# A streaming encoder layer in exact float32 parts: weight parts kept in DRAM, and branch B's v normalised by two passes of the vector engine

## The chip, the core and the metric

The kernel runs on one core of one Trainium2 chip. The metric is the device time of one execution in microseconds (us), as the median of several runs. Five engines share the work of a core: PE multiplies matrices (its weight loads are listed apart, as PEld), DVE is the vector engine, ACT the scalar engine, POOL the GpSimd engine, and SP here only issues DMAs. Each runs its own list of instructions in the order in which the program gives them.

## The reference

One layer of an encoder runs over a new stream of 2048 frames and over eight running streams of 16 frames each, all of width 1024, in float32. What is computed, cut to what matters here:

```python
h = einsum('btd,de->bte', x, w_in)                     # 1024 -> 2816 columns
a, g_a, u, v, g_b, c1, c2, g_c = split(h)              # 256 256 384 384 384 384 384 384
y_a = pool_mixer(a)                                    # trailing means, 4 windows, 64 x 64 products
v_n = layer_norm(v, gmlp_ln_g, gmlp_ln_b)
y_b = u * spatial_mix(v_n, gmlp_w, gmlp_b)             # 4 heads, 128 x 128, lower triangle
c   = c1 * sigmoid(c2)
y_c = silu(layer_norm(conv31(c))) @ conv_pw_w + conv_pw_b    # causal, one filter a channel
mixed = concat(silu(g_a) * y_a, silu(g_b) * y_b, silu(g_c) * y_c)
x_new = layer_norm(2 ** 0.25 * x + mixed @ w_out + b_out)

def layer_norm(x, g, b):
    return (x - mean) * rsqrt(var + 1e-5) * g + b
```

The normalised rows of v of the running streams, and the last rows of a and c, are outputs too.

## The kernel before, in words

**Products in two parts.** PE's one-pass type holds fewer bits than float32. Each operand is therefore split into a high part, which is the cast, and a low part, which is what is left: `split` (L150) has ACT cast (L152), and DVE subtract 1.0 us later by the planner's time. A product is three matmuls (`mm3`, L183): high by high (L189), high by low and low by high (L190, L191).

**Tokens and groups.** The 2048 frames are 16 token tiles of 128; a 17th holds the eight running streams. Three blocks take 6, 6 and 5 of them. The split tokens of a block stay in SBUF (`xhi`, `xlo`; `XRow`, L212, loads and splits one k-tile of 128 rows). The 2816 columns of w_in are done in eight groups, in this order: two of c1 and c2, two of ga and a, then v, gb, u, gc. A group has three column tiles of 128 (those of ga and a two). So the weights of all eight groups are needed again in each block.

**Weights.** A group's weights come in four pieces of two k-tiles each (`Piece`, L166): a load from DRAM into one of four slots of the stage (L171), on SP's DMA queue, and then a split into one of six slots of the weight ring (`whi`, `wlo`). A `Loader` (L799) starts the loads of the next group while the present one runs. It splits the first pieces after 6 and 9 us of planned PE time and two more during the group's last product; each split frees a slot of the stage for the next load. This is done anew in every block. At the end of a block the tokens of the next one come through the same stage.

**Branch B.** For each token tile `b_v` (L627) makes v in PSUM, and `stats` (L363) takes mean and variance on DVE (`vst`, `vmv`). After 1.0 us POOL makes 1/sigma and -mean/sigma out of them (`rstd`, L376: `vrs` in L378 and L379, `vnm` in L381). After another 1.2 us ACT normalises from PSUM into `vn` (L385), and after 0.8 us more POOL multiplies by `vg` (L649) and adds `vb` (L650). Of three tiles together each of the four heads is split (`vhi` on ACT, `vlo` on DVE) and multiplied by the spatial weights (`ps_z`, L672). POOL later multiplies the results `zb` by the gate (L689), and `b_u` (L692) by u, with a transposition (`tp_b`, L706).

**Branch C.** The convolution is 31 taps for each channel tile on DVE, one instruction a tap (`acc`, 128 x 768). Its taps are filler: `run_fill` (L100) puts one into DVE's list wherever the planner's clock of DVE has fallen behind its clock of PE. A block's tail (mean, variance, pointwise product; L496) runs during the next block, and that of the last one during the output stage.

**Branch A** makes its differences on DVE and its 64 x 64 products with split weights (`poolwhi`, `poolwlo`), which are loaded once (L315).

**What sets the order.** Nothing is reordered: each engine runs its instructions as the program gives them (L87 to L131). `after(us, ...)` puts a step into the lists when the planner's clock of PE has come that far. All DVE work but a few steps at the start goes through one wrapper and carries the line L131; it is told apart by its tiles. SP's DMAs start in order too.

**Output stage.** The branches of a token tile are stored to DRAM (`mix`), loaded again and split (`Mixed`, L878), and multiplied by w_out (`WPart`, L898), which takes the place of the tokens. The first two token tiles go together, k by k (`ps_o`). POOL scales b_out (L926) and adds it to the residual rows `xr` (L947); DVE then adds `ps_o` to `xr`.

Of the kernel before, what the change touches and what calls it, by code (L numbers as in the profile page):

```python
# [9 lines left out]
F32 = mybir.dt.float32  # L10
# [15 lines left out]
# Column tiles of 128 of the input projection.  # L26
# [23 lines left out]

# Columns of the packed per-partition constants.
# [22 lines left out]
def encoder_kernel(ctx: ExitStack, tc: tile.TileContext, a):  # L74
# [29 lines left out]
    def drain(tag=None):  # L104
        """What is left of the convolution that `tag` names, or all of it."""
# [13 lines left out]
    class Vector:  # L119
        """The vector engine, with its time counted."""  # L120
# [27 lines left out]
    ring = {}  # L148

    def split(hi, lo, src, then=None):  # L150
        """src (float32) = hi + lo exactly, both in the tensor engine's one-pass type."""
# [14 lines left out]
    class Piece:  # L166
        """A load into the stage, and later its split into a piece of the weight ring."""
        def __init__(self, key, src, cols):
            self.key, self.n, self.cols = key, src.shape[1], cols
# [3 lines left out]
        def split(self, then=None):  # L173
# [3 lines left out]
            ring.setdefault(self.key, []).append((hi, lo))  # L177

# [4 lines left out]
    def mm3(outs, kdim=KT, hook=None):  # L183
        """outs: (ps, lhs, rhs); the products of both parts but for lo x lo, below float32's last bit."""
# [18 lines left out]
    def w_in(key, g):  # L203
        """The loads of a group's weights, to be made one by one."""
# [889 lines left out]
```

## Time and profile before

| | |
|---|---|
| median of 3 runs | 805.1 us (805.04 to 805.83) |
| span of the profiled execution | 802.9 us |
| the three runs' median less this span | 2.2 us |
| PE busy | 778.2 us, 97% |
| DVE busy | 659.0 us, 82% |
| ACT busy | 255.0 us, 32% |
| POOL busy | 216.7 us, 27% |
| DMA | 88.34 MB, 110 GB/s on average |

The profile is one execution, and its times count from the start of the span. A row for a single instruction gives its start, its length, the engine, the line, the operation with output and inputs, and in square brackets the idle time before it and the work that ended this idle time. A row with a count (x4) holds several alike that follow each other, with their busy time together. A row of a group gives count, busy time, mean length in ns and the idle time before its members. In a list of waits the engine that waited stands ahead of the arrow, and the one it waited for behind it. A busy share near 100% says that an engine is hardly ever without work; it does not say what its short pauses wait for.

### The profile page before, as it was taken

How to read it: one execution, taken by the hardware profiler on the slowest of the kernel's cores; microseconds unless marked ns; L12 is line 12 of the kernel's file. 1: busy time of each engine (PE TensorE's matmuls, PEld its weight loads, DVE VectorE, ACT ScalarE, POOL GpSimd, SP SyncE). 2: the span in 40 equal slices, each digit the busy share in tenths (PEclk: the TensorE clock that was granted, in tenths of full speed). 3: DMA queues.
4: the chain of work that ended last, by engine and by line, in shares of the span. 5: the costliest groups of instructions: out<-in, count | busy, mean ns of one | idle time of the engine just before them, and what ended most of it. 6: DMA issues, size and time to landing. Idle time of an engine off the chain costs nothing.

```text
span 802.9 us, 11388 instructions
## 1 busy us (share of the span) xinstructions
PE 778.2 (97%) x4340; PEld 734.9 (92%) x4340; DVE 659.0 (82%) x930; ACT 255.0 (32%) x457; POOL 216.7 (27%) x226
## 2 busy tenths in 40 slices
PE   8999998999999999989999999999999899999995
PEld 6999997999999999989999999999988678888885
DVE  5998989995588999999667888999777897676665
ACT  5313224314432241431354243442351233231210
POOL 1010077300002005731000201742009344232332
PEclk9999999999999999999999999999999999999998
DMA  7513311225501253111461134222575344425321
GB/s 244 162 53 109 100 60 57 64 66 170 165 28 53 73 133 97 60 40 59 136 199 47 54 83 129 83 69 86 159 236 203 124 138 158 158 108 177 121 79 64
DMA packets 50918, 88.34 MB, mean 110 GB/s; under 512 B 13616, under 2 KB 27440, under 8 KB 50864
## 3 DMA queue, kind: packets, MB, share of 16 engines
q1 hardware_dynamic: 50864, 87.62, 33.9%
q8 instruction: 34, 0.56, 0.3%
q14 instruction: 20, 0.16, 0.1%
HBM read 69.02 MB, written 18.58 MB: 109 GB/s over the span
## 4 chain that ended last, share of the span: by engine, by line
PE 70%; DVE 13%; POOL 6%; issue 4%; DMA 4%; ACT 2%; SPq 0%; POOLq 0%; DVEq 0%; ACTq 0%
PE ps_c L189 6%; PE ps_o L189 5%; PE ps_o L191 5%; PE ps_c L190 5%; PE ps_o L190 5%; PE ps_c L191 5%; DVE acc L131 4%; PE ps_u L191 3%; PE ps_u L189 3%; PE ps_u L190 3%; PE ps_gc L191 2%; PE ps_gc L189 2%; PE ps_gc L190 2%; PE ps_ga L190 2%; PE ps_ga L189 2%
## 5 line engine op out<-in xcount | busy, mean ns | idle before, releaser
L131 DVE SCALAR_TENSOR_TENSOR acc<-cext,cw,acc 128x768 f32<-128x768 f32 (+1 forms) x270 | 265.8, 984 | 4.0
L131 DVE TENSOR_TENSOR wlo<-stage,whi 128x768 fp32r<-128x768 f32 (+1 forms) x99 | 90.0, 919 | 15.8 <-ACT whi L152 15.4
L189 PE MATMUL ps_c<-xhi,whi 128*128 128x384 f32 (+1 forms) x288 | 96.1, 334 | 0.6 <-ACT xhi L152 0.6
L190 PE MATMUL ps_c<-xlo,whi 128*128 128x384 f32 (+1 forms) x288 | 94.7, 329 | 0.9 <-DVE xlo L131 0.9
L191 PE MATMUL ps_c<-xhi,wlo 128*128 128x384 f32 (+1 forms) x288 | 94.1, 327 | 0.0
L152 ACT CAST whi<-stage 128x768 fp32r<-128x768 f32 (+1 forms) x99 | 75.4, 773 | 25.3 <-PE ps_c L190 11.8
L191 PE MATMUL ps_o<-woxhi,mlo 128*128 128x512 f32 (+1 forms) x208 | 81.5, 392 | 1.8 <-DVE mlo L131 1.8
L189 PE MATMUL ps_o<-woxhi,mhi 128*128 128x512 f32 (+1 forms) x208 | 81.9, 394 | 0.0
L190 PE MATMUL ps_o<-woxlo,mhi 128*128 128x512 f32 (+1 forms) x208 | 80.7, 388 | 0.0
L440 POOL COPY halo_c<-cext 128x30 f32<-128x30 f32 x9 | 5.1, 567 | 213.4 <-DVE cext L131 213.4
L190 PEld LDWEIGHTS ps_c<-xlo,whi 128*128 128x128 f32 x288 | 54.4, 189 | 2.4 <-DVE xlo L131 2.4
L189 PEld LDWEIGHTS ps_c<-xhi,whi 128*128 128x128 f32 x288 | 54.5, 189 | 1.4 <-ACT xhi L152 1.2
L191 PEld LDWEIGHTS ps_c<-xhi,wlo 128*128 128x128 f32 x288 | 54.3, 189 | 0.0
L385 ACT ACTIVATE xr<-xr,onm,ors 128x1024 f32<-128x1024 f32 x16 | 19.9, 1244 | 106.3 <-POOL onm L381 106.3
L191 PEld LDWEIGHTS ps_o<-woxhi,mlo 128*128 128x128 f32 x208 | 39.4, 189 | 11.0 <-DVE mlo L131 2.2
L189 PE MATMUL ps_gc<-xhi,whi 128*128 128x384 f32 (+1 forms) x144 | 47.3, 328 | 0.0
L191 PE MATMUL ps_gc<-xhi,wlo 128*128 128x384 f32 (+1 forms) x144 | 47.0, 326 | 0.0
L190 PE MATMUL ps_gc<-xlo,whi 128*128 128x384 f32 (+1 forms) x144 | 46.9, 326 | 0.0
L190 PEld LDWEIGHTS ps_o<-woxlo,mhi 128*128 128x128 f32 x208 | 39.4, 190 | 8.1
L189 PE MATMUL ps_gb<-whi,xhi 128*128 128x384 f32 x136 | 46.8, 344 | 0.0
L189 PE MATMUL ps_u<-whi,xhi 128*128 128x384 f32 x136 | 46.6, 343 | 0.0
L189 PEld LDWEIGHTS ps_o<-woxhi,mhi 128*128 128x128 f32 x208 | 39.6, 190 | 7.5
(188 smaller groups left out, 1967.1 us busy)
## 6 DMA issues: line engine op xcount, KB each, us to landing
stage<-in_w_in SPq DMA_DIRECT2D x71, 384.0 KB, 3.6
xr<-in_x_prompt SPq DMA_DIRECT2D x16, 512.0 KB, 4.9
o_y<-xr SPq DMA_DIRECT2D x16, 512.0 KB, 2.9
stage<-mix SPq DMA_DIRECT2D x17, 384.0 KB, 4.0
stage<-in_w_in SPq DMA_DIRECT2D x24, 256.0 KB, 2.7
stage<-in_xT SPq DMA_DIRECT2D x14, 384.0 KB, 3.8
mix<-yt SPq DMA_DIRECT2D x17, 192.0 KB, 1.9
mix<-mixs SPq DMA_DIRECT2D x17, 192.0 KB, 2.1
```

Of the source, the lines that this page charges most:

```text
L131: return fn(*args, **kw)
L152: nc.scalar.copy(hi, src)
L189: nc.tensor.matmul(ps, lh, rh, start=(k == 0), stop=False)
L190: nc.tensor.matmul(ps, lh, rl, start=False, stop=False)
L191: nc.tensor.matmul(ps, ll, rh, start=False, stop=(k == kdim - 1))
L385: nc.scalar.activation(out=out, in_=src, func=AF.Identity, scale=rs, bias=nm_)
L440: nc.gpsimd.tensor_copy(halo_c[:, j, :], ext[:, Tp:Tp + CONVC])
```

## The change

**Weights.** In block 0 everything is loaded and split as before, but 3 us (planned) after each split the two parts of the piece are also written to DRAM, into tiles named `keep` (`put`: two DMAs on SP, 64 in all). In blocks 1 and 2 a new class `Kept` loads the two parts from there, straight into the weight ring, or, for the first two pieces of every second group, into the stage, two slots a piece, from which PE then reads. Nothing is split there: 44 pieces of 768 columns and 16 of 512 go from ACT (cast) and DVE (subtraction). The loads are issued 5 to 8 us after the start of the group before, those that go into the stage after 10 and 11. Only the last group of the last block is still loaded from w_in and split.

**Tokens.** From block 0 to 1 the token rows still come through a `Loader`; from block 1 to 2 they are loaded during the last products of the block and split partly after its last group.

**v.** On DVE, right behind the statistics, a first pass takes (v - mean) times `vg` from PSUM into `vn`. POOL makes only 1/sigma (`inverse`). After 2.4 us a second pass, on DVE, multiplies by 1/sigma and adds `vb`. ACT's normalisation (17 instructions), POOL's -mean/sigma (17) and POOL's two passes (34) go; DVE has 34 more instructions of 128 x 384.

Since the planner counts DVE's work, taps move into the room that the subtractions leave.

```diff
     class Piece:
-        def __init__(self, key, src, cols):
-            self.key, self.n, self.cols = key, src.shape[1], cols
+        def __init__(self, key, src, cols, keep=None):
+            self.key, self.n, self.cols, self.keep = key, src.shape[1], cols, keep
...
             ring.setdefault(self.key, []).append((hi, lo))
+            if self.keep is not None:
+                after(3, lambda: put(self.keep, hi, lo, self.cols))
+
+    def put(keep, hi, lo, cols):
+        for x, part in enumerate((hi, lo)):
+            nc.sync.dma_start(out=keep[:, x], in_=part[:, :, :cols].bitcast(F32))
+
+    class Kept:
+        def __init__(self, key, k, keep, cols, staged):
+            if staged:
+                parts = [stage().bitcast(F32R).rearrange("p (k c) -> p k c", k=2) for _ in range(2)]
+            else:
+                parts = [core.tile([P, 2, 384], F32R, tag=x, bufs=RING, name=x) for x in ("whi", "wlo")]
+            for x, part in enumerate(parts):
+                nc.sync.dma_start(out=part[:, :, :cols].bitcast(F32), in_=keep[:, x])
+            ring.setdefault(key, [None] * (KT // 2))[k] = tuple(parts)
...
+    after(5, put_first)
     after(12, load_pool)
     after(24, load_v)
...
-    def rstd(mv, nm):
+    def inverse(mv, nm):
         rs = const.tile([P, 1], F32, tag="rs", bufs=4, name=nm + "rs")
         nc.gpsimd.tensor_scalar(rs, mv[:, 1:2], 1.0, EPS, op0=ALU.mult, op1=ALU.add)
         nc.gpsimd.tensor_tensor(out=rs, in0=rs, in1=mhalf, op=ALU.pow)
+        return rs
...
-                def norm(rs, nm_, o=vn[:, r, :], ps=ps):
-                    normalise(o, ps[:, :384], rs, nm_)
-                    def gain():
-                        nc.gpsimd.tensor_tensor(out=o, in0=o, in1=vg, op=ALU.mult)
-                        nc.gpsimd.tensor_tensor(out=o, in0=o, in1=vb, op=ALU.add)
-                    after(0.8, gain)
-                stats(lambda _: ps[:, :384], 1, "v", norm)
...
+                o = vn[:, r, :]
+                vec.scalar_tensor_tensor(out=o, in0=ps[:, :384], scalar=mv[:, 0:1], in1=vg,
+                                         op0=ALU.subtract, op1=ALU.mult)
+                rs = inverse(mv, "v")
+                after(2.4, lambda o=o, rs=rs: vec.scalar_tensor_tensor(out=o, in0=o, scalar=rs, in1=vb,
+                                                                       op0=ALU.mult, op1=ALU.add))
...
         for g in range(LASTG):
-            loads = Loader([(fn, 1) for fn in w_in((b, g + 1), g + 1)])
-            after(6, loads.next)
-            after(9, loads.next)
-            group_work(b, g, loads.hook({1: 1, 3: 1}))
+            if b == 0 or (b, g + 1) == (LASTB, LASTG):
+                loads = Loader([(fn, 1) for fn in w_in((b, g + 1), g + 1)])
+                after(6, loads.next)
+                after(9, loads.next)
+                group_work(b, g, loads.hook({1: 1, 3: 1}))
+            else:
+                for i, fn in enumerate(w_kept(b, g + 1)):
+                    after(10 + i if g % 2 == 0 and i < 2 else 5 + i, fn)
+                group_work(b, g, None)
```

**The order, place 1: DVE, where block 0's first token tiles of v are made.** `vst` and `vmv` are the statistics, `acc` a tap, `wlo` the subtraction for a weight piece of the next group, and the `vlo` made from `dpool` belongs to branch A. Before:

```order
L131 BN_STATS vst<-ps_v 128x6
L131 BN_AGGR vmv<-vst 128x2
L131 SCALAR_TENSOR_TENSOR acc_490<-cext_344,cw,acc_490 128x768 x2
L131 TENSOR_TENSOR wlo<-stage,whi 128x768
L131 BN_STATS vst<-ps_v 128x6
L131 BN_AGGR vmv<-vst 128x2
L131 TENSOR_TENSOR vlo<-dpool,vhi 128x384
```

The same place now:

```order
L131 BN_STATS vst<-ps_v 128x6
L131 BN_AGGR vmv<-vst 128x2
L131 SCALAR_TENSOR_TENSOR vn<-ps_v,vmv,vg 128x384
L131 SCALAR_TENSOR_TENSOR vn<-vn,vrs,vb 128x384
L131 SCALAR_TENSOR_TENSOR acc_518<-cext_364,cw,acc_518 128x768
L131 TENSOR_TENSOR wlo<-stage,whi 128x768
L131 BN_STATS vst<-ps_v 128x6
```

The two passes have come in behind the statistics; the second, which needs POOL's `vrs`, follows the first directly here, and one tap less stands ahead of `wlo`.

**A little later on DVE, where the first spatial products of block 0 are prepared** (`vlo` from `vn`, for the first two heads), with instance numbers. Before:

```order
L131 TENSOR_TENSOR vlo_1197<-vn_964,vhi_1196 128x288
L131 TENSOR_TENSOR wlo_1203<-stage_959,whi_1202 128x768
L131 TENSOR_TENSOR wlo_1218<-stage_961,whi_1217 128x768
L131 TENSOR_TENSOR vlo_1223<-vn_964,vhi_1222 128x288
L131 BN_STATS vst_1245<-ps_v_1192 128x6
```

The same place now:

```order
L131 TENSOR_TENSOR vlo_1252<-vn_1026,vhi_1251 128x288
L131 TENSOR_TENSOR wlo_1258<-stage_1021,whi_1257 128x768
L131 SCALAR_TENSOR_TENSOR vn_1155<-vn_1155,vrs_1244,vb_186 128x384
L131 TENSOR_TENSOR wlo_1268<-stage_1023,whi_1267 128x768
L131 TENSOR_TENSOR vlo_1273<-vn_1026,vhi_1272 128x288
```

Between the two `vlo` the two weight subtractions have stayed, and a second pass has come in.

**Place 2: SP, in block 0's first group.** Before, the pool weights (`pw`) came right behind the weight loads that follow the constants `cst`:

```order
L272 DMA cst<-in_cst 128x151
L171 DMA stage<-in_w_in 128x768 x4
L315 DMA pw_320<-in_pool_w 64x64 x4
L171 DMA stage<-in_w_in 128x512 x4
L297 DMA vg<-in_gmlp_ln_g 128x384
```

Now:

```order
L172 DMA stage<-in_w_in 128x768 x4
L184 DMA keep_2_92<-whi 128x768
L184 DMA keep_2_92<-wlo 128x768
L184 DMA keep_4_93<-whi 128x768
L184 DMA keep_4_93<-wlo 128x768
L184 DMA keep_6_94<-whi 128x768
L184 DMA keep_6_94<-wlo 128x768
L184 DMA keep_0_91<-whi 128x768
L184 DMA keep_0_91<-wlo 128x768
L184 DMA keep_0_218<-whi 128x768
L184 DMA keep_0_218<-wlo 128x768
L349 DMA pw_338<-in_pool_w 64x64 x4
```

Ten stores, those of the first five pieces, now stand ahead of the pool weights; each waits for its part of the piece.

**Place 3: DVE, where the output stage begins.** `woxlo` and `wlo` are the last low parts of w_out, `acc` taps of the last block's third channel tile, and `xr` takes up the first products `ps_o`. Before:

```order
L131 TENSOR_TENSOR woxlo_5926<-stage,woxhi_5925 128x768 x2
L131 TENSOR_TENSOR wlo<-stage,whi 128x512
L131 SCALAR_TENSOR_TENSOR acc_4441<-cexts,cw,acc_4441 128x128
L131 SCALAR_TENSOR_TENSOR acc_4441<-cext_4281,cw,acc_4441 128x512
L131 SCALAR_TENSOR_TENSOR acc_4441<-cexts,cw,acc_4441 128x128
```

There are 25 such rows of taps there, and then the first `xr`. Now:

```order
L131 TENSOR_TENSOR woxlo_5876<-stage,woxhi_5875 128x768 x2
L131 TENSOR_TENSOR wlo<-stage,whi 128x512
L131 SCALAR_TENSOR_TENSOR xr<-xr,ps_o 128x512 x4
L131 BN_STATS ost<-xr 128x6 x2
L131 BN_AGGR omv<-ost 128x2
```

The 25 rows have moved ahead of this place, and `xr` follows the last `wlo` directly.

More of the change, by code (lines that the diff above doesn't have):

```diff
@@ L206, in w_in, with w_kept, put_first @@
         v = a["w_in"][:, gofs[g]:gofs[g] + KT * w].rearrange("p (k c) -> p k c", k=KT)
-        return [lambda k0=k0: Piece(key, v[:, k0:k0 + 2, :], w) for k0 in range(0, KT, 2)]
+        if key[0] == 0:
+            kept[g] = [dram.tile([P, 2, 2, w], F32, name=f"keep{g}_{k0}") for k0 in range(0, KT, 2)]
+        keep = kept[g] if key[0] == 0 else [None] * (KT // 2)
+        return [lambda k0=k0: Piece(key, v[:, k0:k0 + 2, :], w, keep[k0 // 2]) for k0 in range(0, KT, 2)]
+    kept = {}
+    def w_kept(b, g):
+        w = len(GROUPS[g]) * P
+        return [lambda k=k: Kept((b, g), k, kept[g][k], w, g % 2 == 1 and k < 2) for k in range(KT // 2)]
+    def put_first():
+        hi, lo = ring[0, 0][0]
+        put(kept[0][0], hi, lo, 384)
     xhi = [None] * (KT // 2)
@@ L643, in b_v @@
                     hook=hook if i + r == len(tiles) - 1 else None)
[L645 to L652 removed]
+                st = const.tile([P, 1, 6], F32, tag="st1", bufs=4, name="vst")
+                vec.bn_stats(out=st[:, 0, :], in_=ps[:, :384])
+                mv = const.tile([P, 2], F32, tag="mv", bufs=4, name="vmv")
+                vec.bn_aggr(out=mv, in_=st.rearrange("p a b -> p (a b)"))
+                o = vn[:, r, :]
[4 more added lines that the diff above has]
+                                                                       op0=ALU.mult, op1=ALU.add))
             if sample:
@@ L852, in encoder_kernel, with leave, load @@
         for g in range(LASTG):
-            loads = Loader([(fn, 1) for fn in w_in((b, g + 1), g + 1)])
-            after(6, loads.next)
-            after(9, loads.next)
-            group_work(b, g, loads.hook({1: 1, 3: 1}))
-        if b < LASTB:
-            W = [(fn, 1) for fn in w_in((b + 1, 0), 0)]
-            X = [(lambda k=k: XRow(b + 1, k), 1) for k in range(KT)]
-            loads = Loader(W[:2] + X[:1] + W[2:3] + X[1:3] + W[3:] + X[3:])
-            group_work(b, LASTG, loads.hook({1: 1, 2: 1, 3: 2, 4: 2, 5: 2, 6: 2}))
-            loads.next(3)
-            X = None
+            if b == 0 or (b, g + 1) == (LASTB, LASTG):
[7 more added lines that the diff above has]
+                group_work(b, g, None)
+        if b == 0:
+            W = w_kept(b + 1, 0)
+            after(5, W[0])
+            after(6, W[1])
+            loads = Loader([(lambda k=k: XRow(b + 1, k), 1) for k in range(KT)])
+            def leave(k):
+                if k in (2, 4):
+                    W[1 + k // 2]()
+                if 2 <= k < 7:
+                    loads.next()
+            group_work(b, LASTG, leave)
+            loads.next(3)
+        elif b < LASTB:
+            for i, fn in enumerate(w_kept(b + 1, 0)):
+                after(5 + i, fn)
+            rows = {}
+            def load(*ks, b=b):
+                for k in ks:
+                    rows[k] = XRow(b + 1, k)
+            def leave(k):
+                if k in (2, 4):
+                    load(k - 2, k - 1)
+                if k == 5:
+                    for i in range(2):
+                        rows[i].split(lambda i=i: load(i + 4))
+            group_work(b, LASTG, leave)
+            for i in range(2, 4):
+                rows[i].split(lambda i=i: load(i + 4))
+            for i in range(4, KT):
+                after((2.5, 3.5, 5.5, 6.5)[i - 4], lambda i=i: rows[i].split())
     flush()
```

2 lines of the change are left out of this document (added).

## The prediction, on record before the changed kernel was run

> **What bounds the kernel now.** I read the page's first part, then the waits of TensorE (PE), then the stretches in which PE loses time, then what is late there.
>
> ```profile
> span 802.9 us, 11388 instructions
> PE 778.2 (97%) x4340; PEld 734.9 (92%) x4340; DVE 659.0 (82%) x930; ACT 255.0 (32%) x457; POOL 216.7 (27%) x226
> 40.00:60.00 20.00, 20.00 (x117) 20.00 (x116) 19.46 (x24) 2.74 (x5) 3.46 (x4) 1.00 0.18 50
> ```
>
> PE is the bound: where nothing stops it, it runs 117 matmuls of 384 columns in 20 us, 171 ns each, and the change touches none of them. A gain can only be time that PE now waits, or runs at a lower clock. The waits of PE in the whole span (who waits, for whom: us in total, times, longest), the waits that ended three of them, and five stretches (length, then busy time of PE, PEld, DVE, ACT, POOL, granted clock, DMA share, GB/s):
>
> ```profile
> PE ps_z L672 <- DVE vlo L131: 6.6, 9, 1.9
> PE ps_var L538 <- DVE csqs L131: 2.1, 1, 2.1
> PE ps_o L191 <- DVE mlo L131: 1.8, 1, 1.8
> PE ps_rstd L561 <- ACT crs L555: 1.5, 1, 1.5
> PE ps_z L672 <- ACT vhi L152: 0.8, 1, 0.8
> PE tp_b L706 <- DVE yb L131: 0.5, 1, 0.5
> ...
> 139.66 0.54 PE L672 MATMUL ps_z<-vlo,wsthi 128*128 128x288 f32 x1 [1.88 <-DVE vlo L131]
> ...
> 120.00:140.00 20.00, 15.89 (x87) 14.57 (x87) 18.16 (x18) 9.13 (x19) 14.63 (x14) 0.99 0.17 48
> 139.80:143.20 3.40, 3.40 (x12) 3.40 (x13) 3.40 (x5) 1.21 (x3) 1.62 (x1) 0.50 0.63 206
> 320.00:360.00 40.00, 36.93 (x214) 35.72 (x213) 38.27 (x42) 15.50 (x31) 24.13 (x24) 1.00 0.18 58
> 500.00:520.00 20.00, 19.83 (x116) 19.55 (x115) 19.32 (x31) 7.67 (x14) 14.36 (x19) 1.00 0.25 75
> 655.20:658.60 3.40, 3.40 (x10) 2.62 (x9) 3.37 (x8) 0.97 (x3) 1.53 (x4) 0.50 1.01 305
> ```
>
> So PE loses 4.1 us in block 0 at the spatial products ps_z (20 less 15.89), 3.1 us at those of block 1, 0.2 at those of block 2 and 0.5 at tp_b, then 5.4 us in the output stage (2.1 + 1.8 + 1.5). Twice the clock stands at 0.50 for 3.4 us, each time right after such a wait: 1.7 us lost each. In all 16.7 us can be won.
>
> What is late at ps_z? On POOL and DVE in block 0's v stage (start, us, idle before and its releaser):
>
> ```profile
> 114.39 0.67 ACT L385 ACTIVATE vn<-ps_v,vnm,vrs 128x384 f32<-128x384 f32 x1 [5.79 <-POOL vnm L381]
> 119.76 0.67 ACT L385 ACTIVATE vn<-ps_v,vnm,vrs 128x384 f32<-128x384 f32 x1 [4.70 <-POOL vnm L381]
> ...
> 120.85 0.97 DVE L131 TENSOR_TENSOR vlo<-vn,vhi 128x288 fp32r<-128x288 f32 x1 [2.18 <-ACT vhi L152]
> 121.75 2.64 DVE L131 TENSOR_TENSOR wlo<-stage,whi 128x768 fp32r<-128x768 f32 x2
> ...
> 26.86 4.18 DVE L131 SCALAR_TENSOR_TENSOR acc<-cext,cw,acc 128x768 f32<-128x768 f32 x4
> ...
> 128.40 8.22 DVE L131 SCALAR_TENSOR_TENSOR acc<-cext,cw,acc 128x768 f32<-128x768 f32 x6
> ...
> 139.17 0.45 DVE L131 TENSOR_TENSOR vlo<-vn,vhi 128x288 fp32r<-128x288 f32 x1
> ```
>
> Each token tile passes POOL (vrs, vnm), ACT, then POOL twice more, one tile after the other: 119.76 - 114.39 = 5.4 us a tile, where PE needs 24 x 0.171 = 4.1. The queue runs late, ACT casts vhi behind it, and DVE stands 2.18 us idle before vlo, then does two weight subtractions ahead of the next.
>
> **The change part by part.** The costliest operations that go, and two that stand for the new ones (count, busy us, mean ns, idle before):
>
> ```profile
> L131 DVE TENSOR_TENSOR wlo<-stage,whi 128x768 fp32r<-128x768 f32 x71 | 70.9, 1010 | 14.1 <-ACT whi L152 13.7
> L131 DVE TENSOR_TENSOR wlo<-stage,whi 128x512 fp32r<-128x512 f32 x28 | 19.1, 688 | 1.7 <-ACT whi L152 1.7
> L650 POOL TENSOR_TENSOR vn<-vn,vb 128x384 f32<-128x384 f32 x17 | 21.3, 1254 | 1.3
> L649 POOL TENSOR_TENSOR vn<-vn,vg 128x384 f32<-128x384 f32 x17 | 20.3, 1196 | 13.4 <-ACT vn L385 13.4
> L131 DVE SCALAR_TENSOR_TENSOR dc<-ps_mean,acc 128x384 f32<-128x384 f32 x15 | 7.4, 551 | 10.4 <-PE ps_mean L518 10.4
> L131 DVE TENSOR_TENSOR csum<-csum,acc 128x384 f32<-128x384 f32 x5 | 2.8, 558 | 0.2
> ```
>
> *Sums of work.* 44 pieces of 768 and 16 of 512 are no longer split: DVE saves 44 x 1.010 + 16 x 0.688 = 55.4 us, all in blocks 1 and 2 and at their starts. DVE gains 34 passes of about 0.555 us, 18.9 us. POOL loses 41.6 us of vg and vb. None of this is on PE's path by itself; the fill lets the convolution's taps move up into the time. What counts is what it does at the waits.
>
> *Block 0, ps_z: 5.8 us of loss (4.1 and 1.7), of which I give back 4.8.* The weights of block 0 are still split, so DVE's order stays full; but the v passes no longer cross POOL twice, and vn is ready long before vlo: the 2.18 us go. The six taps at 128.40 took 1.37 us each, beside POOL's last vn passes and the zb products after them, against 1.05 for the four at 26.86, where POOL stood still; the zb products stay, so of these 2 us about half come back. With the 2.18 us of idle time that go earlier in the same queue that covers the 1.88 us that PE waited at 139.66. What stays: between the first and the second vlo DVE does two subtractions and a second pass, 1.0 + 0.55 + 1.0 + 0.45 = 3.0 us, while PE comes back for the next product after nine matmuls and the product's own three, 2.0 us: 1.0 us of wait. New is that a second pass, on DVE itself, waits for vrs (two POOL operations); behind it stand vlo, taps and subtractions. Where a tap lies between, the wait is covered; where none does (the first tile, in the order shown above) DVE idles about 1 us, and three such tiles could add up to 3 us of lateness: bounds of the gain 1.7 (the clock alone) and 5.8. The Trainium skill (SBUF — State Buffer, section "SBUF: two separate sides") says that VectorE and GpSimd lock one port pair for a whole instruction. By it the passes, with two SBUF inputs, could also hold up the POOL operations that they wait for; the 1.37 us taps agree with the lock.
>
> The clock term rests on the two rows at 0.50, each behind a wait of 1.9 us or less. The Trainium skill (TensorE: Matmul & The Clock Gate, "Part 1") says that the clock halves after an idle window of about 3.4 us. By that neither wait would have done it, and removing them would give no clock back: the sum below would be 3.4 us smaller.
>
> *Block 0, the stores: -2.0.* Each piece is now also written out, in two DMAs on SP, each the size of the piece's load (first row). At the start this is in the way: ten stores come ahead of the pool weights on SP's queue.
>
> ```profile
> stage<-in_w_in SPq DMA_DIRECT2D x71, 384.0 KB, 3.6
> 22.39 3.09 SPq L315 DMA_DIRECT2D pw<-in_pool_w  x4
> 34.16 0.42 DVE L131 TENSOR_TENSOR poolwlo<-pw,poolwhi 128x256 fp32r<-128x256 f32 x1
> 57.09 0.69 DVE L131 TENSOR_TENSOR wlo<-stage,whi 128x512 fp32r<-128x512 f32 x1 [0.23 <-ACT whi L152]
> 58.49 0.33 PE L189 MATMUL ps_ga<-xhi,whi 128*128 128x384 f32 x1
> 0.00:20.00 20.00, 17.35 (x78) 13.72 (x79) 10.51 (x16) 10.17 (x14) 2.33 (x15) 1.00 0.77 245
> ```
>
> Ten stores are 3.9 MB, and two loads (0.8 MB) are still under way at 22.4. At the 305 GB/s of the full stretch quoted above that is 15.5 us, so the pool weights land near 40 and poolwlo starts some 6 us after 34.16. DVE stands still for that, with taps, cext and the weights of the next group behind it. The group at 58.49 needs its last piece after 18 matmuls, at 61.6; it is ready at 57.09 + 0.69 = 57.8: 3.8 us of cover. PE then waits about 2 us. Ends: 0, if DVE's idle time swallows it, and 6.4 at the 245 GB/s of the first 20 us.
>
> *Blocks 1 and 2, ps_z and tp_b: +2.8 and +0.2.* No weight subtraction stands between the vlo any more, and the POOL chain is gone; of 3.1 us I leave 0.3, of 0.7 us 0.5. Bounds 0 and 3.8. Weights come 3.1 MB a group; a group of three tiles lasts 144 x 0.171 = 24.6 us, so 128 GB/s, under half of 305, and they are asked for a group ahead: nothing. At the start of block 2 the token rows are loaded only when the stage is free of the last group's weights, 0 to 1 us.
>
> *Output stage: 7.1 us of loss (5.4 and 1.7), of which +5.3.* DVE's last taps, 25 instructions, stood between the last wlo and the first xr; the order now has none. POOL was hurt by them too:
>
> ```profile
> 602.63 9.34 POOL L926 TENSOR_SCALAR b_out<-b_out 128x1024 f32<-128x1024 f32 x1 [55.47 <-DMA b_out<-in_b_out]
> 612.05 7.16 POOL L947 TENSOR_TENSOR xr<-xr,b_out 128x1024 f32<-128x1024 f32 x3
> 614.49 1.28 DVE L131 SCALAR_TENSOR_TENSOR xr<-xr,ps_o 128x512 f32<-128x512 f32 x2 [3.44 <-POOL xr L947]
> 616.87 1.28 DVE L131 SCALAR_TENSOR_TENSOR xr<-xr,ps_o 128x512 f32<-128x512 f32 x2 [1.09 <-POOL xr L947]
> 588.60 0.39 PE L189 MATMUL ps_o<-woxhi,mhi 128*128 128x512 f32 x1
> 588.83 0.39 PE L190 MATMUL ps_o<-woxlo,mhi 128*128 128x512 f32 x1
> ```
>
> The scaling of b_out took 9.34 us while DVE ran taps; an xr addition of the same width, with two inputs, takes 7.16 / 3 = 2.4. With DVE idle I give b_out at most that: the first xr is ready at 607.4 and DVE waits for PE, whose 96 matmuls at 0.23 us from 588.6 end at 610.7. DVE starts xr 3.6 us sooner than 614.49. The three waits that follow add up to 5.4, all behind DVE's queue; 3.6 of them go, 1.8 stay, spread, and the clock's 1.7 go. Bounds 0 and 7.1.
>
> Sum: 4.8 - 2.0 + 2.8 + 0.2 + 5.3 = 11.1 us off the profiled span, 791.8. The three timed runs have a median of 805.1, 2.2 above the span; I keep that: 794.0.
>
> **The rivals.** *DVE stays late in the v stage (0.18).* The waits for vrs and the taps in the fill keep DVE behind, so that ps_z waits as before in blocks 0 and 1 and only its clock loss goes: gain 11.1 - 3.1 - 2.8 = 5.2, 799.9. For it: DVE is busy 19.46 of 20 us at 40 to 60. Against: in the v stage it was idle, waiting for ACT.
>
> *The clock's two halvings stay (0.06).* They would then not hang on these waits but come back wherever PE is briefly idle, as it still is in this forecast: 11.1 less both 1.7 is 7.7, 797.4. Against: both rows at 0.50 stand right behind a wait, and the longest wait left is 1.0 us in block 0. This is also what the page on the clock gate, of the Trainium skill, would make of it.
>
> *All of it goes (0.09)*: no wait left, stores hidden: 805.1 - 16.7 = 788.4.
>
> *Nothing comes of it (0.07).* DVE stays late in the v stage and the output stage's waits return behind ACT and POOL (ps_rstd waited for ACT): 5.2 - 5.3 = -0.1, 805.2.
>
> *The stores become the bound of block 0 (0.11), slower.* Its eight groups take 6 x 24.6 + 2 x 16.4 = 180 us and move 11.5 MB in and 23.1 MB out, 34.6 MB. The rate from which this loses against the 8.3 us gained elsewhere is 34.6 / (180 + 8.3 + 1.6) = 182 GB/s; at 170 the block takes 203.5, and the result is 805.1 + 23.5 - 8.3 = 820. For it: one queue, whose stores wait for DVE and hold loads behind them. Against: 245 GB/s over the first 20 us.
>
> **How the numbers follow.** Forecast 0.49. The range runs from 787 (all gained, less the 1.4 us that such small waits are uncertain by) to 802 (the first rival and 2 us of the stores' bound); it leaves out most of the last two cases, 0.18. Faster by over 0.2% (1.6 us, about what a measurement can tell from no change): 0.49 + 0.18 + 0.06 + 0.09 = 0.82; within it 0.07; slower 0.11.
>
> **What would show it.** Right: PE's wait for vlo falls from 6.6 us to under 2; no stretch at 0.50 near the first ps_z; b_out on POOL under 3 us; the first xr on DVE right after PE; poolwlo near 40 and a PE wait near 60 us. Wrong: vlo still on top of PE's waits, a wait of PE for whi or wlo at group starts in block 0, DVE waiting for vrs by microseconds, or xr still waiting for POOL.

## The result, and the profile after

The changed kernel takes 785.75 us (median of 4 runs, 785.06 to 785.92), the kernel before in the same job 805.07 (4 runs, 804.99 to 805.83). The ratio is 0.9761, with a 95% interval of 0.9747 to 0.9776: 19.3 us faster. The forecast was 794.0 and its range ended at 787, so it had the direction and lay outside on the fast side: it gave the change 11.1 us, little more than half of what it brought. The first part of the page after:

```profile
span 784.2 us, 11348 instructions
PE 771.1 (98%) x4340; PEld 732.4 (93%) x4340; DVE 611.3 (78%) x904; ACT 203.8 (26%) x380; POOL 146.3 (19%) x175
```

All waits of PE after (who waits, for whom: us in total, times, longest):

```profile
PE wps L277 <- POOL wz L274: 1.5, 1, 1.5
PE ps_rstd L600 <- ACT crs L594: 1.1, 1, 1.1
PE tp_b L748 <- ACT yt L750: 0.8, 1, 0.8
PE ps_c L209 <- DVE xlo L131: 0.5, 1, 0.5
PE ps_ga L210 <- DVE wlo L131: 0.4, 1, 0.4
PE ps_c L208 <- ACT xhi L152: 0.4, 1, 0.4
PE ps_o L208 <- ACT sgc L533: 0.3, 1, 0.3
```

The 6.6 us of ps_z behind vlo are gone completely, and of the output stage's three waits one is left, with a short new one behind ACT's sgc. Three stretches of the windows view after (length, then busy time of PE, PEld, DVE, ACT and POOL with the number of instructions, granted clock, DMA share, GB/s):

```profile
120.00:140.00 20.00, 20.00 (x121) 20.00 (x121) 18.04 (x24) 8.60 (x19) 4.61 (x5) 1.00 0.63 217
320.00:360.00 40.00, 40.00 (x238) 40.00 (x237) 37.51 (x41) 8.62 (x20) 9.91 (x9) 1.00 0.43 155
0.00:198.60 198.60, 195.79 (x1118) 191.77 (x1119) 170.00 (x214) 61.61 (x105) 24.11 (x45) 1.00 0.71 243
```

Compare the counts in brackets with the rows of before. From 120 to 140 PE did 87 matmuls before and 121 now; from 320 to 360 it did 214 and now 238. The last row is block 0: its DMAs ran at 243 GB/s and behind the start it lost PE time at one place, at 59.6 us.

Where the 18.7 us of the two spans come from is read from the first matmul of each stage, in the traces of the two profiled executions (us; a stage ends where the next row's tile begins):

| stage | before | after | gained | forecast |
|---|---|---|---|---|
| start to the first ps_ga, block 0 | 58.49 | 57.30 | 1.19 | 0 |
| ps_ga to ps_v, block 0 (stores) | 34.33 | 35.06 | -0.73 | -2.0 |
| ps_gb to ps_u, block 0 (ps_z) | 35.43 | 28.27 | 7.16 | +4.8 |
| the same, block 1 | 32.45 | 28.27 | 4.18 | } +2.8 |
| the same, block 2 | 27.37 | 26.73 | 0.64 | } |
| ps_u to ps_gc, block 2 (tp_b) | 23.12 | 23.38 | -0.26 | +0.2 |
| first ps_o to the last matmul | 205.95 | 199.73 | 6.22 | +5.3 |
| last matmul to the end | 8.35 | 8.07 | 0.28 | 0 |

Of the 7.6 us by which the spans gained more than the 11.1 of the forecast, 2.4 stand at ps_z of block 0, 2.0 at ps_z of the other two blocks, 0.9 in the output stage, 1.3 at the stores and 1.2 at the start; the rest makes -0.2. The row of the start is mostly chance: in the other profiled kernels of this study that stage took 57.2 to 58.1 us, with the same program there but for the stores. The two medians differ by 0.6 us more than the spans. In every run whose span is listed the time is 1.7 to 1.8 us above the span, so the profiled execution before, at 802.9, was some 0.5 us faster than the median of its kernel: of the 2.2 us that the forecast kept, 1.7 lie around the span.

### The profile page after: what moved, and what is told of

Same layout as the page of the kernel before. It is cut to its first block, busy times and chain, and to the rows that moved or that the text cites. A ratio compares the mean times of both kernels' runs of the same rounds, so it can differ in the third digit from the quotient of the medians.

```text
span 784.2 us, 11348 instructions
## 1 busy us (share of the span) xinstructions
PE 771.1 (98%) x4340; PEld 732.4 (93%) x4340; DVE 611.3 (78%) x904; ACT 203.8 (26%) x380; POOL 146.3 (19%) x175
## 4 chain that ended last, share of the span: by engine, by line
PE 87%; DVE 3%; DMA 3%; SPq 3%; ACT 1%; POOL 1%; issue 1%; POOLq 0%; DVEq 0%; ACTq 0%
PE ps_o L208 7%; PE ps_o L210 7%; PE ps_o L209 7%; PE ps_c L208 4%; PE ps_c L210 4%; PE ps_c L209 4%; PE ps_gb L208 3%; PE ps_gb L209 3%; PE ps_gb L210 3%; PE ps_v L209 3%; PE ps_v L210 3%; PE ps_v L208 3%; PE ps_u L210 3%; PE ps_u L209 3%; PE ps_u L208 3%; PE ps_gc L210 2%
## 5 line engine op out<-in xcount | busy, mean ns | idle before, releaser
L208 PE MATMUL ps_c<-xhi,whi 128*128 128x384 f32 (+1 forms) x240 | 79.7, 332 | 0.4 <-ACT xhi L152 0.4
L209 PE MATMUL ps_c<-xlo,whi 128*128 128x384 f32 (+1 forms) x240 | 79.1, 329 | 0.5 <-DVE xlo L131 0.5
L210 PE MATMUL ps_c<-xhi,wlo 128*128 128x384 f32 (+1 forms) x240 | 78.5, 327 | 0.0
L131 DVE TENSOR_TENSOR xlo<-stage,xhi 128x768 fp32r<-128x768 f32 (+2 forms) x26 | 21.6, 853 | 35.5 <-ACT xhi L152 35.5
L210 PE MATMUL ps_u<-whi,xlo 128*128 128x384 f32 x136 | 45.6, 335 | 0.0
L209 PE MATMUL ps_u<-wlo,xhi 128*128 128x384 f32 x136 | 45.5, 335 | 0.0
L209 PE MATMUL ps_v<-wlo,xhi 128*128 128x384 f32 x136 | 45.5, 334 | 0.0
L210 PE MATMUL ps_v<-whi,xlo 128*128 128x384 f32 x136 | 45.5, 334 | 0.0
L208 PE MATMUL ps_v<-whi,xhi 128*128 128x384 f32 x136 | 45.5, 334 | 0.0
L131 DVE TENSOR_TENSOR xr<-xr,ln_g 128x1024 f32<-128x1024 f32 x16 | 28.5, 1782 | 20.1 <-ACT xr L424 20.1
```

The source lines that it names most:

```text
L131: return fn(*args, **kw)
L208: nc.tensor.matmul(ps, lh, rh, start=(k == 0), stop=False)
L209: nc.tensor.matmul(ps, lh, rl, start=False, stop=False)
L210: nc.tensor.matmul(ps, ll, rh, start=False, stop=(k == kdim - 1))
```

## The experiments

The question was why so much more came than was forecast, and which part brings it. Theory A is the forecast's: the POOL chain makes vlo late at ps_z, and the subtractions that go let the taps leave the output stage. Rival B is DVE's load: what counts everywhere is the 55 us of subtractions that go, and the new passes only cost. Ratios are against the kernel before in the same job, with their 95% intervals.

**The norm alone.** The kernel before, with the change's two passes, which the planner isn't told of (`nc.vector` in place of the wrapper `vec`):

```diff
-                stats(lambda _: ps[:, :384], 1, "v", norm)
+                nc.vector.scalar_tensor_tensor(out=o, in0=ps[:, :384], scalar=mv[:, 0:1], in1=vg,
+                                         op0=ALU.subtract, op1=ALU.mult)
+                rs = inverse(mv, "v")
+                after(2.4, lambda o=o, rs=rs: nc.vector.scalar_tensor_tensor(out=o, in0=o, scalar=rs, in1=vb,
```

> The kernel before with only the v norm of the change (two DVE passes, POOL keeps 1/sigma); weights are loaded and split in every block as before, and the planner is not told of the 34 passes, so that every tap stands where it stood. Theory A (the POOL chain made ps_z wait): from the first ps_gb to the first ps_u of block 0 the time falls from 35.4 us to 28.3-29.5, as in the changed kernel (28.3); in block 1 from 32.4 to 28.5-30, though splits are still there; the output stage keeps its 205.9 us from the first ps_o to the last matmul, or a little more, since DVE has 19 us more to do. Total 794 to 797. Rival B (it is DVE's load: the subtractions that go make the gain everywhere, the new passes only cost): block 0 and 1 stay at 33-36 and 31-33, total 804 to 809.

Measured: 802.78 us (before 804.59), ratio 0.9979 (0.9968 to 0.9989). From ps_gb to ps_u block 0 took 30.99 us and block 1 30.07, so the POOL chain is part of it, as A says. But PE still waited for vlo, block 2 got slower (29.46), and so did the output stage (207.68). Neither theory had this total. DVE's list just ahead of the second vlo, block 0:

```profile
113.64 2.06 DVE L131 SCALAR_TENSOR_TENSOR acc<-cext,cw,acc 128x768 f32<-128x768 f32 x2
115.62 0.61 DVE L658 SCALAR_TENSOR_TENSOR vn<-vn,vrs,vb 128x384 f32<-128x384 f32 x1
116.15 2.07 DVE L131 SCALAR_TENSOR_TENSOR acc<-cext,cw,acc 128x768 f32<-128x768 f32 x2
...
119.48 1.01 DVE L131 SCALAR_TENSOR_TENSOR acc<-cext,cw,acc 128x768 f32<-128x768 f32 x1
120.41 0.45 DVE L131 TENSOR_TENSOR vlo<-vn,vhi 128x288 fp32r<-128x288 f32 x1
120.77 0.95 DVE L131 TENSOR_TENSOR wlo<-stage,whi 128x768 fp32r<-128x768 f32 x1
121.64 0.61 DVE L658 SCALAR_TENSOR_TENSOR vn<-vn,vrs,vb 128x384 f32<-128x384 f32 x1
122.17 0.95 DVE L131 TENSOR_TENSOR wlo<-stage,whi 128x768 fp32r<-128x768 f32 x1
123.04 0.45 DVE L131 TENSOR_TENSOR vlo<-vn,vhi 128x288 fp32r<-128x288 f32 x1
```

The same place in the changed kernel:

```profile
113.26 1.01 DVE L131 SCALAR_TENSOR_TENSOR acc<-cext,cw,acc 128x768 f32<-128x768 f32 x1
114.19 0.61 DVE L131 SCALAR_TENSOR_TENSOR vn<-vn,vrs,vb 128x384 f32<-128x384 f32 x1
114.72 1.01 DVE L131 SCALAR_TENSOR_TENSOR acc<-cext,cw,acc 128x768 f32<-128x768 f32 x1
...
116.99 1.01 DVE L131 SCALAR_TENSOR_TENSOR acc<-cext,cw,acc 128x768 f32<-128x768 f32 x1
117.91 0.45 DVE L131 TENSOR_TENSOR vlo<-vn,vhi 128x288 fp32r<-128x288 f32 x1
...
120.55 0.46 DVE L131 TENSOR_TENSOR vlo<-vn,vhi 128x288 fp32r<-128x288 f32 x1
```

Between the same instructions stand three taps in place of five, and the first vlo starts 2.5 us sooner, though PE began with v 0.5 us later. The planner knows there of 1.1 us of passes a tile and gives DVE fewer taps. So the change has a third part, which the diff doesn't show as one: that the passes are counted.

**The kept weights alone.** The changed kernel with the old norm:

```diff
-                vec.scalar_tensor_tensor(out=o, in0=ps[:, :384], scalar=mv[:, 0:1], in1=vg,
-                                         op0=ALU.subtract, op1=ALU.mult)
...
+                stats(lambda _: ps[:, :384], 1, "v", norm)
```

> The changed kernel with the old norm of v (ACT normalises, POOL multiplies by vg and adds vb); the weight parts are still kept in DRAM. Theory A: block 0 from ps_gb to ps_u stays near 35 us (33-36), block 1 between 29 and 32 because the POOL chain is back but no subtraction stands between the vlo; the output stage has its whole gain (199-200 us in place of 205.9). Total 793 to 797. Rival B (DVE's load alone): block 1 and 2 as in the changed kernel, 28.3 and 26.7, output 199.7; total 788 to 793 with block 0 alone unhelped.

Measured: 797.55 us (before 804.59), ratio 0.9917 (0.9903 to 0.9931). The output stage took 198.64 us: its whole gain, 7.3. The ps_z stages gained nothing to speak of: 35.42, 31.67 and, in block 2, 28.39. With no subtraction between the vlo of block 1, PE waits there all the same. B falls for ps_z and holds for the output stage.

**The changed kernel with the passes not counted**, to test the third part:

```diff
-                vec.scalar_tensor_tensor(out=o, in0=ps[:, :384], scalar=mv[:, 0:1], in1=vg,
+                nc.vector.scalar_tensor_tensor(out=o, in0=ps[:, :384], scalar=mv[:, 0:1], in1=vg,
...
-                after(2.4, lambda o=o, rs=rs: vec.scalar_tensor_tensor(out=o, in0=o, scalar=rs, in1=vb,
+                after(2.4, lambda o=o, rs=rs: nc.vector.scalar_tensor_tensor(out=o, in0=o, scalar=rs, in1=vb,
```

> The changed kernel, but the planner is not told of the 34 passes of DVE; so taps are put in as if the passes took no time. Theory A2 (what the norm alone left in block 0, 30.99 us in place of 28.27, comes from the taps that the planner puts ahead of vlo when it does not count the passes): block 0 from ps_gb to ps_u about 31, or 34 where the clock halves; block 1 about 30; block 2 28 to 29.5; the output stage stays at 199-200. Total 791 to 797. Rival A1 (the rest came from the subtractions of blocks 1 and 2, or from the place of POOL's work, and the planner's count does nothing): 28.3 in both, total 785 to 787.

Measured: 794.48 us (before 804.45), ratio 0.9877 (0.9861 to 0.9892). Block 0 took 34.53 us, the clock at half for 6.8 of them, and block 1 30.99; PE waited 5.9 us for vlo. Not to count the passes costs 8.7 us, by medians of two jobs whose kernels before took 804.45 and 805.07.

**The norm alone, counted.** The first kernel of this section with the wrapper `vec`, and the tail of the last block started at the third output tile:

```diff
-TAILQ = 9
+TAILQ = 2
...
-                nc.vector.scalar_tensor_tensor(out=o, in0=ps[:, :384], scalar=mv[:, 0:1], in1=vg,
+                vec.scalar_tensor_tensor(out=o, in0=ps[:, :384], scalar=mv[:, 0:1], in1=vg,
```

> The kernel before with the new norm, and the planner told of its passes; since more taps are left for the output stage, the tail of the last block starts at the third output tile whatever is left. Theory A2: block 0 from ps_gb to ps_u 28.3 to 29, block 1 28.3 to 29.5, as in the changed kernel; the output stage pays for it (39 tap rows ahead of the first xr in place of 31, and 4 behind): 209 to 214 us in place of 205.9. Total 797 to 803. Rival A1: block 0 stays at 31 or above, total 801 to 808.

Measured: 797.96 us (before 804.45), ratio 0.9917 (0.9901 to 0.9933). All three ps_z stages are those of the changed kernel: 28.27, 28.27, 26.73, though every weight piece is still split in every block and the subtractions still stand between the vlo. The output stage paid: 211.84 us. Its windows for the two stretches, and PE's longest wait:

```profile
120.00:140.00 20.00, 20.00 (x122) 20.00 (x121) 17.15 (x22) 8.58 (x19) 4.61 (x5) 1.00 0.23 71
320.00:360.00 40.00, 40.00 (x237) 40.00 (x236) 37.33 (x43) 13.68 (x28) 9.97 (x9) 1.00 0.20 60
...
616.93 0.79 PE L191 MATMUL ps_o<-woxhi,mlo 128*128 128x512 f32 x1 [6.51 <-DVE mlo L131]
```

The taps that are held back at ps_z come out in the output stage, ahead of the first xr and mlo. Kept weights give DVE the room to do them earlier: from here to the changed kernel the output stage falls by 12.1 us (211.84 to 199.73), and nothing else by more than 0.8. That the tail starts earlier here may have a share in the 211.84; no run separates it.

**The old norm, counted as if it were the new.** Is it then the norm at all, or only that taps are held back? The kept weights with the old norm, and planner's time for passes that nobody makes:

```diff
                 stats(lambda _: ps[:, :384], 1, "v", norm)
+                Clock.dve += 0.55
+
+                def count():
+                    Clock.dve += 0.55
+                after(2.4, count)
```

> The kept weights with the old norm, and the planner is told of two passes a tile that DVE doesn't make (0.55 us each, at the places of the new passes), so that it holds taps back as in the changed kernel. Theory A (the POOL chain, some 5.4 us a tile, makes vhi and vlo late whatever DVE does): block 0 from ps_gb to ps_u 33-36 us, as with the old norm uncounted (35.4); block 1 30-32; total 793 to 798. Rival H (only the taps ahead of vlo made it late, and the norm itself is not what counts): 28.3 to 29 in both blocks, total 785 to 788.

Measured: 791.35 us (before 804.64), ratio 0.9837 (0.9817 to 0.9857). Block 0 took 32.22 us, block 1 29.55, block 2 26.73: just below A's range at both blocks, and above H's. Both halves are real. DVE and POOL there, ahead of the first vlo of block 0:

```profile
115.08 0.99 DVE L131 SCALAR_TENSOR_TENSOR acc<-cext,cw,acc 128x768 f32<-128x768 f32 x1
120.44 0.98 DVE L131 TENSOR_TENSOR vlo<-vn,vhi 128x288 fp32r<-128x288 f32 x1 [4.38 <-ACT vhi L152]
```

```profile
115.56 1.38 POOL L688 TENSOR_TENSOR vn<-vn,vg 128x384 f32<-128x384 f32 x1 [0.79 <-ACT vn L424]
117.02 1.02 POOL L689 TENSOR_TENSOR vn<-vn,vb 128x384 f32<-128x384 f32 x1
118.12 0.19 POOL L413 TENSOR_SCALAR vrs<-vmv 128x1 f32<-128x1 f32 x1
```

With fewer taps DVE stands idle for 4.4 us before vlo: here it is the POOL chain that is late. From tile to tile it pauses only for ACT's vn, 0.79 us each time.

**What the stores cost.** First the norm alone (not counted) with the 64 stores of block 0, which nobody reads; blocks 1 and 2 run the loop of the kernel before:

```diff
-                for i, fn in enumerate(w_kept(b, g + 1)):
-                    after(10 + i if g % 2 == 0 and i < 2 else 5 + i, fn)
-                group_work(b, g, None)
+            loads = Loader([(fn, 1) for fn in w_in((b, g + 1), g + 1)])
+            after(6, loads.next)
+            after(9, loads.next)
+            group_work(b, g, loads.hook({1: 1, 3: 1}))
```

> The run with the norm alone, and in block 0 the 64 stores of the weight parts, which nobody reads: blocks 1 and 2 load and split as before. What it is slower by than the norm alone is what the stores cost. The forecast had 2.0 us at the group of ga (PE waiting for weights near 60 us). By the trace of the changed kernel (one wait of 0.4 us there, 0.7 us by the matmuls' pitch): +0.4 to +1.2 us. Rival C (stores are free, what is seen near 60 us is chance): within 0.3 us of the norm alone.

Measured: 805.05 us (before 804.59), ratio 1.0006 (0.9991 to 1.0020), 2.3 above the norm alone. The profiled execution had no wait near 60 us; its extra time stands at ps_z of block 0 (34.44 against 30.99), where PE waited 3.3 us for vlo and the clock then stood at half for 6.8 us. DVE's wait for the pool weights, and the first vlo from vn:

```profile
36.71 0.42 DVE L131 TENSOR_TENSOR poolwlo<-pw,poolwhi 128x256 fp32r<-128x256 f32 x1 [2.68 <-ACT poolwhi L152]
122.01 0.45 DVE L131 TENSOR_TENSOR vlo<-vn,vhi 128x288 fp32r<-128x288 f32 x1
```

In the norm alone DVE had no such wait, and with the same 54 taps ahead of it the first vlo started at 120.41 (at 121.97 where the passes are not counted, which has the stores too). So what DVE loses to the stores at 37 us is carried along its queue and paid where DVE has no slack. The granted clock says the same of the other runs: its mean is 0.991 over the 12 runs here and 0.994 over the 11 of the norm alone, by estimate 2 us of time. What the stores cost the changed kernel, whose DVE has slack at ps_z, the next kernel asks: the changed one with the pool weights loaded ahead of all stores.

```diff
-    after(12, load_pool)
+    after(2, load_pool)
```

> The changed kernel with the pool weights loaded ahead of all stores (issued 2 us after the start in place of 12). Theory F (the forecast's step: the stores make the pool weights late, and DVE's wait for them makes PE wait near 60 us, 0.7 us by the pitch of the matmuls): the wait goes, -0.5 to -0.8 us, 785.0 to 785.3. Rival G (DVE is behind there in any case, 19.6 us busy of 20): no change within 0.3 us, or the wait moves to another piece.

Measured: 784.88 us (784.67 to 785.29; before 804.45), ratio 0.9761 (0.9745 to 0.9778). The wait near 60 us is gone and the stage from ps_ga to ps_v back at 34.33 us. But this doesn't show that the pool weights made the wait. Five other profiled kernels run the changed kernel's program, late pool weights included, up to that place (the kept weights alone, the norm with stores, the passes not counted, the old norm counted, and the stops that follow below). In them DVE waited 2.3 to 2.8 us for the pool weights, in place of 3.47, and that stage took 34.33 to 34.41 us. Against the kernels before of their own jobs the changed kernel and this one have the same ratio, 0.9761. So the stores cost the changed kernel 0.7 us in one profiled execution of six and at most 0.1 in the others, not 2.0; F and G aren't told apart.

Each part stored twice (`keep` twice as large) shows how far the stores are from more:

```diff
             nc.sync.dma_start(out=keep[:, x], in_=part[:, :, :cols].bitcast(F32))
+            nc.sync.dma_start(out=keep[:, 2 + x], in_=part[:, :, :cols].bitcast(F32))
```

> The changed kernel with each part stored twice in block 0, the second copy read by nobody: 46.2 MB out and 11.5 in. At the 331 GB/s of the stretch from 20 to 40 us of the changed kernel 57.7 MB take 174 us, block 0 lasts 194. Theory D (there is room, the queue only has to reach that rate): +1 to +4 us, most of it near 60 us where the pool weights come later still. Rival E (the queue with its stores waiting for DVE reaches no more than the 245 GB/s of the first 20 us): 57.7 MB take 236 us, +30 to +45 us. Whichever, it shows how far the stores are from being block 0's bound.

Measured: 800.63 us (before 804.59), ratio 0.9955 (0.9939 to 0.9970): about 15 us more than the changed kernel, between D and E. All of it is from ps_ga to ps_v in block 0 (51.28 us in place of 35.06). There SP's list puts loads behind stores, at 52.26 us where the changed kernel issued them at 37.82, and PE runs dry. From 40 to 80 us, and SP's rows at that place:

```profile
40.00:60.00 20.00, 19.38 (x112) 18.92 (x110) 10.53 (x14) 2.43 (x5) 1.41 (x2) 1.00 0.89 335
60.00:80.00 20.00, 7.56 (x23) 6.73 (x24) 17.20 (x21) 3.14 (x6) 1.70 (x4) 0.57 0.85 272
```

```profile
42.05 3.84 SPq L350 DMA_DIRECT2D pw<-in_pool_w  x4
...
51.26 0.95 SPq L185 DMA_DIRECT2D keep<-wlo  x1
52.26 2.93 SPq L172 DMA_DIRECT2D stage<-in_w_in  x4
```

The mean rate over 20 to 120 us was 342 GB/s, so E's 245 is not the queue's limit, and at that rate the block's 57.7 MB take 169 us: as a whole block 0 has room. What binds is its start, where the stores of two groups stand ahead of the loads of the third in a queue that already runs at such a rate; from ps_v on, every stage was as in the changed kernel to 1.0 us.

**The clock.** The changed kernel with eleven stops of PE after groups of blocks 1 and 2, added work of no use:

```diff
+    def stop(n):
+        pd = psm.tile([P, 512], F32, tag="mm", name="ps_stop")
+        nc.tensor.matmul(pd[:, :P], onef, ident, start=True, stop=True)
+        sc = tmp.tile([P, 256], F32, tag="stop", name="stop")
+        nc.scalar.copy(sc[:, :P], pd[:, :P])
+        nc.scalar.copy(sc[:, P:], sc[:, :P])
+        for _ in range(n):
+            nc.scalar.copy(sc, sc)
+        nc.tensor.matmul(pd[:, P:2 * P], onef, sc[:, :P], start=True, stop=True)
...
+                if g != 4:
+                    stop(2 * g + b)
```

> The changed kernel with eleven stops of PE in blocks 1 and 2, each a matmul, some copies on ACT (256 columns, 2 to 14 of them) and a matmul that waits for them: about 1 to 6 us each, growing by about 0.35 us a copy. They are added work of no use. Theory W (the clock is set for a stretch of 3.41 us by the stretch before it, on a fixed grid, and falls to 0.50 where PE was busy for less than about 0.40 of it): every stop that leaves a stretch under 0.40 is followed by 3.4 us at 0.50, stops of 2 to 3 us among them, and those that leave over 0.42 are not. Rival S (a whole stretch of 3.4 us without work is needed): only stops above 3.4 us, and of these not all, are followed by it.

Measured: 850.62 us, one run. Two stops, with the idle time before the second matmul, and the stretches of 3.41 us around them:

```profile
255.29 0.58 PE L874 MATMUL ps_stop<-stop,ones 128*128 128x128 f32 x1 [1.99 <-ACT stop L873]
```

```profile
280.38 0.49 PE L874 MATMUL ps_stop<-stop,ones 128*128 128x128 f32 x2 [3.03 <-ACT stop L873]
```

```profile
251.86:255.27 3.41, 1.44 (x10) 1.25 (x8) 2.56 (x4) 1.80 (x6) 1.00 (x2) 1.00 0.65 178
255.27:258.69 3.42, 3.40 (x11) 3.40 (x12) 2.23 (x3) 1.09 (x2) 0.00 (x0) 0.50 0.95 294
275.75:279.16 3.41, 1.61 (x10) 1.41 (x9) 3.27 (x4) 1.86 (x6) 1.00 (x1) 1.00 0.00 0
279.17:282.58 3.41, 2.20 (x13) 2.20 (x14) 1.63 (x2) 1.10 (x3) 0.20 (x1) 1.00 0.00 0
```

The stop of 1.99 us halves the clock and the longer one of 3.03 us doesn't: the first lies in one stretch of the grid, the second is shared by two. Of the eleven stops those of 1.99 and 2.43 us and all six from 3.42 us up were followed by 0.50, those of 1.28, 1.68 and 3.03 us were not. S falls, and W's grid holds. W's bound, a busy share of about 0.40, does not: in the kernel before, the stretch from 651.77, with PE busy for 1.88 of 3.41 us, was followed by 0.50, and the one at 275.75 here, busy for 1.61, was not. The last section counts streamed columns in place of busy time.

**A faster version.** The pool weights first, and one more step of the tail between the variance and its use in the output stage:

```diff
             yield lambda: variance(i, t0, n)
             yield None
+            if b == LASTB and i == 0:
+                yield None
...
-            after(6, lambda tail=tail: spread(tail, 4.4))
+            after(6, lambda tail=tail: spread(tail, 4.2))
```

> The run with the pool weights ahead, and in the output stage one more step of the tail between variance and its use in the first half (steps 4.2 us apart in place of 4.4). PE's wait for ps_rstd, 1.5 us by the pitch, goes: -1.2 to -2.2 us against the changed kernel, 783.5 to 784.5. Rival: the wait returns at another step of the tail, since the steps are closer: 785 to 787.

Measured: 783.47 us (783.2 to 783.9; before 804.45), ratio 0.9742 (0.9726 to 0.9759). PE's wait for ps_rstd is gone, and the output stage takes 197.76 us. It beats both kernels.

## Why the prediction fell short

**Put together.** Against before, the kept weights alone bring 7.0 us (797.55 against 804.59). Counting two passes, with the old norm still in place, brings 6.2 more (791.35), and the norm itself another 5.6 (785.75, from another job; the kernels before of the two jobs differ by 0.4). The parts aren't independent: the norm counted gains all there is at ps_z and loses 5.9 us of it in the output stage (its tail started earlier there, too); the kept weights are what takes that loss away.

**The sizing of the loss failed first.** "In all 16.7 us can be won" was summed from busy time that was missing and from waits. A matmul's row lasts 0.33 us where one starts every 0.171, and the row behind a wait is drawn longer still (0.44 at 60.33 in the last rows of this section): so busy time covers a part of every pause. The rows that the forecast quoted had the answer in their counts. From 120 to 140 us stood 87 matmuls where 117 fit: 30 x 0.171 = 5.1 us, not 4.1; from 320 to 360 stood 214, with two times 117 possible: 20 x 0.171 = 3.4 and by the stages 4.2, not 3.1. At ps_z of block 0 the stages give 7.16 us, 5.5 without the clock's 1.7. In the output stage the forecast's 5.4 us was what the waits added up to; by the starts of the matmuls they cost 5.9 (1.9, 2.3 and 1.7). With 0.6 in block 2, 0.7 at tp_b and the clock's 3.4 that is some 20 us to be won, 805.1 - 20 = 785, and the end of the range at 787 was no bound.

**Block 0, ps_z: given 4.8, measured 7.16.** The step that failed is "What stays: between the first and the second vlo ... 1.0 us of wait". The distance was right, 2.64 us after against the 3.0 of the forecast. But the first vlo came early enough: it ended at 118.36, and PE took it up at 119.56. PE's rows for the first two heads after:

```profile
119.42 0.29 PE L714 MATMUL ps_z<-vhi,wsthi 128*128 128x288 f32 x1
119.56 0.30 PE L714 MATMUL ps_z<-vlo,wsthi 128*128 128x288 f32 x1
...
121.53 0.30 PE L714 MATMUL ps_z<-vlo,wsthi 128*128 128x288 f32 x1
```

The lead of 1.2 us covers what the second vlo is slower by, 2.64 us against the 1.97 in which PE comes back. It comes from the held-back taps: the forecast took it that "DVE's order stays full" and didn't ask what the planner does with 1.1 us more a tile. Of the new wait of the second pass for vrs, for which the forecast feared up to 3 us, 0.2 came, once.

**Blocks 1 and 2: given 2.8, measured 4.8, for a wrong reason.** "No weight subtraction stands between the vlo any more" isn't it: the norm counted has them there and loses nothing, and the kept weights alone haven't and PE waits. At tp_b, given 0.2, nothing was won: PE waits 0.8 us there for ACT, where it waited 0.5 for DVE.

**The output stage: given 5.3, measured 6.2, for the right reason.** The first xr came right behind PE, and b_out no longer beside taps; on DVE and POOL after:

```profile
597.18 1.30 DVE L131 SCALAR_TENSOR_TENSOR xr<-xr,ps_o 128x512 f32<-128x512 f32 x2 [9.19 <-PE ps_o L210]
```

```profile
590.41 1.05 POOL L1000 TENSOR_SCALAR b_out<-b_out 128x1024 f32<-128x1024 f32 x1 [56.83 <-DMA b_out<-in_b_out]
```

From the first ps_o to xr it is 20.8 us in place of 25.9. The forecast had 3.6 of these 5.1 (3.8 by its own 614.49 - 610.7). The 0.23 us that it took for each of the 96 matmuls was right, but it let xr wait for the last of them: the first xr started right after the 87th, which ended at 597.07, 2.1 us ahead of the 96th.

**The stores: given -2.0, measured -0.7 once and -0.1 at most in five other executions.** poolwlo started at 37.56 where "near 40" was forecast, and DVE stood 3.47 us idle for it. PE's wait came where it was expected, at 60 us, but was short; with 2.3 to 2.8 us of idle time on DVE it did not come. The cover of 3.8 us was nearly enough, or enough:

```profile
37.56 0.42 DVE L131 TENSOR_TENSOR poolwlo<-pw,poolwhi 128x256 fp32r<-128x256 f32 x1 [3.47 <-ACT poolwhi L152]
...
60.33 0.44 PE L210 MATMUL ps_ga<-xhi,wlo 128*128 128x384 f32 x1 [0.43 <-DVE wlo L131]
```

**The rivals.** The one that came nearest is "all of it goes" (788.4), given 0.09, and its price was too small by the sizing above. That the stores bind block 0 did not happen, and doubling them showed where they would: at its start, by what stands behind them in the queue, and not over the whole block, as the rival was priced. The clock went as forecast, both halvings with their waits.

## What to carry to other kernels

Size what can be won by counting the starts of the bounding engine's instructions, or by the time from one stage's first instruction to the next stage's, not by missing busy time or listed waits. Where a planner fills an engine by its own clock, an edit that it counts also moves the filler: ask what the order does with the time it now sees. A small wait in one profile should be looked for in every other profile that runs the same program there, before it is given a cause. And a change in two parts can be worth more than the sum of them, where one part holds work back and the other makes the room in which it is done.

## What the runs showed of the hardware

**The clock goes by activity on a fixed grid.** Where a trace has several stretches at 0.50, they begin at multiples of 3.413 us from each other (in the norm counted, for one, at 614.11 and 638.00 us, seven times that). Taken over the twelve traces, with a stretch's activity as the columns that PE streamed in it (about 7,700 at 384 columns in 0.171 us): after every one of the 18 stretches at full clock with under 2,850 columns the next was halved, after none with over 3,130, and of five between 2,880 and 3,080 after two. A pause of 2 us that falls into one stretch is enough; one of 3 us across two isn't. The Trainium skill (TensorE: Matmul & The Clock Gate, "Part 1") has the free-running window of 3.4 us, and the traces agree; it puts the clock's fall behind an idle window, and here a window with over a third of its columns does it. The kernel before, with its waits of about 2 us, spread from 801.88 to 806.99 us over 23 runs, the changed one from 785.06 to 785.92 over four. Halvings that a run has or hasn't, 1.7 us each, are not the whole of that: runs of 802.72 and of 806.41 us both have a mean granted clock of 0.995, where one halving is worth 0.002.

**POOL beside DVE: one waits for the other.** The scaling of b_out took 1.05 us with DVE idle, less than the 2.4 that the forecast allowed. In the profile of before it took 9.34 us beside DVE's taps, and ended 0.92 us after the last of them. That taps run beside it isn't enough, though: in three other kernels (the norm alone, with stores, and counted) DVE's taps ran without a gap too, and it took 1.22, 1.59 and 1.40 us. There the taps gave way. In the norm counted a tap of 128x128, 0.34 us long elsewhere, took 2.49 us beside the additions to xr, of 2.4 to 2.9 us each:

```profile
592.81 7.68 POOL L954 TENSOR_TENSOR xr<-xr,b_out 128x1024 f32<-128x1024 f32 x3 [2.47 <-DMA xr<-in_x_prompt]
```

```profile
592.91 2.49 DVE L131 SCALAR_TENSOR_TENSOR acc<-cexts,cw,acc 128x128 f32<-128x128 f32 x1
595.33 2.89 DVE L131 SCALAR_TENSOR_TENSOR acc<-cext,cw,acc 128x512 f32<-128x512 f32 x1
598.14 2.49 DVE L131 SCALAR_TENSOR_TENSOR acc<-cexts,cw,acc 128x128 f32<-128x128 f32 x1
```

The Trainium skill (SBUF — State Buffer, section "SBUF: two separate sides") has the two engines lock one port pair for a whole instruction; the taps that last as long as the additions agree with it, though no run here separates the lock from other causes. Why POOL in the profile of before stood back for 18 taps in a row, no run here shows.
